# Early loads reordered over two queues, residual stores on GpSimd's queue, rotary products and low parts on VectorE in a two-layer decoder step

## The chip, the cores and the metric

The kernel runs on one core of one Trainium2 chip. The metric is the device time of one execution in microseconds (us). The engines are PE (TensorE), DVE (VectorE), ACT (ScalarE), POOL (GpSimd) and SP (SyncE, which only issues transfers here). An engine runs its instructions in one fixed row; a transfer is issued by an engine (SP, ACT or POOL), and an instruction that waits holds up everything behind it in that engine's row.

## The reference

One step of a decoder with two layers on 1024 prompt tokens and 8 sequences of 4 new tokens, 1056 tokens in all, with a model width of 1024, in float32. Layer 0 mixes by multi-head latent attention, where the 32 new tokens also attend over 8192 past positions each, held in pages of 128 rows that a table names. Layer 1 mixes by a gated delta rule with a short convolution. Each layer ends with a SwiGLU network.

```python
def rmsnorm(x, w): ...            # x * rsqrt(mean(x*x) + eps) * w
def mla_core(q_lat, q_rope, rows, q_pos, k_pos):      # 8 heads, latent rows of 256 + 64
    s = (einsum('bqhr,bkr->bhqk', q_lat, c) + einsum('bqhp,bkp->bhqk', q_rope, kr)) * MLA_SCALE
    p = softmax(where(k_pos <= q_pos, s, -inf))
    return einsum('bhqk,bkr->bqhr', p, c)
def mla_out(o_lat, w_uv, w_o):
    o = einsum('bthr,hrv->bthv', o_lat, w_uv).reshape(b, t, 1024)
    return o @ w_o
def dn_mixer(...):                # u @ w_in, convolution of width 4, silu, l2norm of q and k,
    ...                           # chunked or recurrent gated delta rule over 8 heads,
    o = rmsnorm(o, g_out) * silu(z)
    return o.reshape(b, t, 1024) @ w_o, s, new_conv
def swiglu(u, w_in, w_out):       # 2816 hidden channels
    gu = u @ w_in
    return (silu(gu[..., :D_FF]) * gu[..., D_FF:]) @ w_out
# each layer: h += rmsnorm(mixer(rmsnorm(h))); h += rmsnorm(swiglu(rmsnorm(h)))
# past rows of the new tokens: cache_mla[j, page_table]
```

## The kernel before

**Products.** Activations lie with channels on the 128 partitions and tokens along the free dimension; the 1056 tokens are three column groups, `GRP`, of 384, 384 and 288. `gA` is the first two, `gB` the last. Every float32 product is made of three matmuls (`mm3`, L255 to L257): both factors are split into a high part, copied by ACT (L230), and a low part, the difference, on DVE (L231) or, where `lo_eng` says so, on POOL. A raw weight `w` is fetched by `raw_weight` (L237) on the queue that `self.queue` names, and split into `wh` and `wl`.

**Order of the work.** PE's row is the order in which the code is written (`self.order()`), and in one block POOL's row is too. The rows of the other engines come from a scheduler, and buffer sets ("pools", `scope`) decide which earlier tile a new tile's place belonged to, and so what a load waits for.

**Layer 0.** Projections with the rotary turn (`rotate`: L604 cos on DVE, L605 sin on POOL, L606 sum on DVE; `swap` fetches the swapped halves) and the attention of the prompt run to about 437 us. Attention writes its heads `oT` to memory. Then three things go together on PE: the decode attention over the pages (`Decode`: `scores` at L1750 and L1754, softmax at L1773, `turn` at L1789, `values` at L1806; a page's part 0 is 128x256, part 1, which the scores read, 128x320), the output projection `wo_half` over `gA`, whose operands `oh` and `ol` are the heads read back (halves of 128x768), and the first network `ffn_half` over `gA`. It runs to about 1200 us. The same stages for `gB`, with `mla_values` first, take until about 1580 us.

**Early loads.** In the block whose POOL row is written by hand, the first loads for all this stand: two weights, the pages of the first two decode steps (`pages(step, part, first, last)`, two transfers a page tile) and the heads. A place can be loaded when the attention is through with it. Later pages are fetched one step ahead, part 0 by POOL and part 1 by SP (L1721).

**Boundaries.** Between sublayers `boundary` takes a column group of sums `acc`, eight tiles: it fetches the residual block `hld` (L327, `NHL` = 3 buffers), scales and adds (L328, L329), stores the new residual from ACT's queue (L331), squares (L385, L389), yields to other work `1 + self.slack` times, sums the squares on PE (L406) and makes the next operands (L336, L337).

**Layer 1.** From about 1580 to 2410 us run the delta rule's eight heads. Each takes four input weights, whose low parts POOL makes (32 in all), a convolution (L1378) and a chain of small operations on DVE up to `kd` (L1668), which PE transposes (L1670). The output projection and the second network follow, to 3230 us.

Of the kernel before, what the change touches and what calls it, by code (L numbers as in the profile page):

```python
# [8 lines left out]
F32 = mybir.dt.float32  # L9
# [3 lines left out]
ALU = mybir.AluOpType  # L13
AX = mybir.AxisListType

P = 128
# [20 lines left out]
LSTEP = 4  # L37
NHL = 3
ABANK = dict(ps=1, sc=4, tp=2, po=1)
# [14 lines left out]
FIRST = 0, 3, 6  # L54
TA = GRP[2][0]
RATE = 0.55
BLK = [(i * P, min(P, T - i * P)) for i in range((T + P - 1) // P)]
# [12 lines left out]
class Two:  # L70
# [16 lines left out]
    def load(self, eng, src, halves=(0, 1)):  # L87
        for i in halves:
            t = self.half(i)
            eng.dma_start(t.bitcast(F32), src[:, (0, TA)[i]:(TA, T)[i]])  # L90

# [10 lines left out]
class K:  # L102


    def __init__(self, ctx, tc, I, O):
# [4 lines left out]
        self.pace, self.ticks = 1, 0  # L110
        self.queue = tc.nc.sync
        self.job_bank = "ps"
# [25 lines left out]
    def half(self, pool, i, dt, s, n=16):  # L138
        return pool.tile([P, (TA, T - TA)[i]], dt, tag="H", bufs=n, name=self.nm(s))

# [172 lines left out]
    def boundary_group(self, g, acc, h_src, h_dst, post, pre, u, sq, full):  # L313
# [10 lines left out]
        for k, a in enumerate(acc):  # L324
            if post is not None:
                h = self.work([P, 384], "hld", NHL)
                nc.sync.dma_start(h[:, :tn], h_src[k][:, s])  # L327
                nc.vector.scalar_tensor_tensor(a, a, self.norm_col(*post, k), r1[:, :tn], op0=ALU.mult, op1=ALU.mult)  # L328
                nc.vector.tensor_tensor(a, a, h[:, :tn], op=ALU.add)  # L329
                if h_dst is not None:  # L330
                    nc.scalar.dma_start(h_dst[k][:, s], a)  # L331
            if full:
# [7 lines left out]
        if not full:  # L340
            return
        for _ in range(1 + self.slack):
            yield 1
# [37 lines left out]
    def sumsq1(self, sums, a, tn, tag, apart=False):  # L381

        new = apart or not sums
        q = self.work([P, 384], tag if new else "sq1")
        self.nc.scalar.activation(q[:, :tn], a, AF.Square)  # L385
        if new:
            sums.append(q)
        else:
            self.nc.vector.tensor_tensor(sums[-1][:, :tn], sums[-1][:, :tn], q[:, :tn], op=ALU.add)  # L389
# [99 lines left out]
    def ffn_half(self, layer, u, r2, acc, gs, end, flush=None, full=()):  # L489
# [3 lines left out]
        def epilogue(g, p, a, hid):  # L493
# [7 lines left out]
            if g not in full:  # L501
                x = a[:, :tn] if gate else self.fp.tile([P, 384], F32, tag="fb", bufs=2, name=self.nm("fb"))[:, :tn]
                nc.vector.tensor_tensor(x, p[:, :tn], r2[:, s], op=ALU.mult)
# [97 lines left out]
    def rotate(self, raw, sw, cos, sin):  # L601

        nc = self.nc
        nc.vector.tensor_tensor(raw, raw, cos, op=ALU.mult)  # L604
        nc.gpsimd.tensor_tensor(sw, sw, sin, op=ALU.mult)  # L605
        nc.vector.tensor_tensor(raw, raw, sw, op=ALU.add)  # L606
# [27 lines left out]
    def first_layer(self, right, top, h1, h2):  # L634
# [4 lines left out]
        with ExitStack() as left:  # L639
# [23 lines left out]
            with self.banks(**DBANK):  # L663
                with self.order(mybir.EngineType.Pool):
# [4 lines left out]

                    def heads(eng, *hs, ds=(0, 1)):  # L670
                        for h in hs:
                            for d in ds:
                                eng.dma_start(uo[h][d].half(0).bitcast(F32), oT[h][d][:, :TA])
# [10 lines left out]
                    heads(nc.gpsimd, 0, ds=(1,))  # L684
                    pages(0, 0, 2, 4)
                    pages(1, 0, 0, 4)
                    pages(0, 0, 0, 1)
                    heads(nc.gpsimd, 0, ds=(0,))
                    heads(nc.sync, 6, 7)
                    for _ in range(2):  # L690
# [21 lines left out]
        self.ab = [None, top.enter_context(self.scope("ab", "right"))]  # L712
        with self.weights(*FW[1], side="left"), self.order(), self.banks(ps=8), self.scope("ffn", "right") as self.fp:
            self.queue = nc.gpsimd
            for h, x in enumerate(uo):
                for d in range(2):
                    nc.sync.dma_start(x[d].half(1)[:, :TP - TA].bitcast(F32), oT[h][d][:, TA:])
            next(steps)
            with self.scope("vals") as vals:
                self.mla_values(OL, uo, vals)  # L720
            with self.scope("ab") as self.ab[0]:
                self.wo_half(uo, acc, gB, start)
                for _ in steps:
                    pass
                for _ in self.ffn_half(0, u, r2, hid, gB, end, full=full):
                    pass
        self.kstep, self.pace, self.queue = KSTEP[0], 1, nc.sync
        return out[:2]
# [17 lines left out]

    def mla_values(self, OL, uo, wk):

        nc = self.nc
        ws = [wk.tile([P, 512], F32, tag="uv", bufs=4, name=self.nm("uv")) for _ in range(4)]  # L750
        for p, w in enumerate(ws):
            nc.sync.dma_start(w, self.I["mla_w_uv"][p])
        for h4 in (0, 4):
            ps = self.psum()
            for k in range(2):
                for e in range(4):
                    h = h4 + e
                    nc.tensor.matmul(ps[e * TS_:(e + 1) * TS_, :P], OL[:, k * 256 + h * TS_:k * 256 + (h + 1) * TS_],
                                     ws[h // 2][:, k * 256 + h % 2 * P:][:, :P], start=k == 0, stop=k == 1)
            t = wk.tile([P, P], F32, tag="ov", bufs=2, name=self.nm("ov"))  # L760
            nc.scalar.activation(t, ps[:, :P], AF.Copy)
# [668 lines left out]
    def dn_vz(self, h, st, u, r2, wk):  # L1430
# [6 lines left out]
        for c0 in (0, 4, 8):  # L1437
# [246 lines left out]
class Decode:  # L1684
# [24 lines left out]

    def load(self, i, part, c0, c1):  # L1710

        self.get(self.early[i], part, c0, c1, self.nc.gpsimd, mybir.EngineType.Pool)

    def get(self, step, part, c0, c1, eng, engine):
        I, (qd, t), (x, n) = self.k.I, step, PGP[part]
        tab = self.tab.rearrange("o (b p) -> o b p", b=DB)[:, 4 * qd + c0:4 * qd + c1, 2 * t:2 * t + 2]
        _, pages = self.nc.values_load_multi_w_load_instructions(
            tab, engines=[engine], min_val=0, max_val=I["cache"].shape[0] - 1,
            skip_runtime_bounds_check_because="the table's entries are pages of the pool")
        for i, page in enumerate(pages):  # L1720
            eng.dma_start(self.pages[step, part][c0 + i // 2][:, i % 2],  # L1721
                          I["cache"][bass.ds(page, 1)].rearrange("o p x -> (o p) x")[:, x:x + n])

    def fetch(self, part):

        if self.coming[part]:
            step = self.coming[part].pop(0)
            self.take(step, part)
            eng = (self.nc.gpsimd, mybir.EngineType.Pool), (self.nc.sync, mybir.EngineType.SP)
            self.get(step, part, 0, 4, *eng[part])  # L1730

# [213 lines left out]
```

## Time and profile before

| | |
|---|---|
| time, median of 3 runs | 3236.57 us (3231.89 to 3242.09) |
| profiled execution | 3232.45 us, span 3230.8 us, mean granted clock 0.975 |
| busy: PE / DVE / ACT / POOL | 3057.4 / 1836.3 / 1173.7 / 564.8 us |
| transfers | 432.42 MB, mean 134 GB/s |
| page loads (L1721) on POOL | 528, 549 ns of POOL each |
| low parts of 1024 columns on POOL, 1580 to 2410 us | 32, 2429 ns each |
| residual stores on ACT (L331) | 48, 192 KB in the wide groups |

Busy times are sums over the span; PE's share of 95% leaves 173 us in which it does nothing. In the rows that follow, a group reads: line, engine, operation, out<-in, then busy time and mean of one, then the idle time ahead of them with what ended it. In a row of waits the numbers are microseconds in all, times, and the longest. In a timeline the first two numbers are start and duration.

### The profile page before, as it was taken

To read this page: it belongs to the slowest core of one execution; us is meant where nothing else is said; L and a number is where in the kernel's file an instruction comes from. 1 tells how busy PE (TensorE), PEld (TensorE's weight loads), DVE (VectorE), ACT (ScalarE), POOL (GpSimd) and SP (SyncE) were. 2 spreads that over 40 slices of the span, in tenths; PEclk is the share of its full clock that TensorE was granted. 3 is DMA by queue.
4 is the path that set the end of the run, shared out by engine and by line. 5 is a ranking of instruction groups with operands and counts; after the bars stand their busy time and mean duration, and the time that the engine had idled before them with its cause. 6 is when DMAs were issued, how large, how long until landed. Compare 5 with 4: busy or idle time off the path is not lost.

```text
span 3230.8 us, 57792 instructions
## 1 busy us (share of the span) xinstructions
PE 3057.4 (95%) x21526; PEld 2805.5 (87%) x21526; DVE 1836.3 (57%) x4197; ACT 1173.7 (36%) x2547; POOL 564.8 (17%) x898
## 2 busy tenths in 40 slices
PE   8899969899999999999999999999899999999998
PEld 8878857788888888999888888888789999999997
DVE  6677745634444444796666666666577444444436
ACT  5344434553333323354344444443443111111121
POOL 1310033343334421011122222222000000000000
PEclk9999989999999999999999999999999999999998
DMA  3563269888788844275413222222332111111113
GB/s 121 189 189 100 70 222 303 278 279 270 242 256 281 262 152 161 91 228 176 134 43 87 75 66 56 74 77 57 124 125 88 40 53 42 50 41 52 40 53 108
DMA packets 287355, 432.42 MB, mean 134 GB/s; under 512 B 60449, under 2 KB 223649, under 8 KB 287074
## 3 DMA queue, kind: packets, MB, share of 16 engines
q1 hardware_dynamic: 217986, 271.75, 26.3%
q0 software_dynamic: 42992, 135.10, 13.0%
q10 hardware_dynamic: 26096, 21.86, 2.2%
q8 instruction: 170, 2.79, 0.4%
q14 instruction: 111, 0.91, 0.1%
HBM read 367.59 MB, written 58.30 MB: 132 GB/s over the span
## 4 chain that ended last, share of the span: by engine, by line
PE 77%; DVE 8%; DMA 4%; issue 3%; ACT 3%; SPq 0%; POOL 0%; ACTq 0%; POOLq 0%; DVEq 0%
PE ps L255 20%; PE ps L256 19%; PE ps L257 19%; PE po L1806 2%; PE sc L1750 2%; DVE y L1378 1%; PE tp L1054 1%; PE sc L1027 1%; DMA hld<-xT 1%; PE sc L1754 1%; PE sc L1021 1%; ACT ga L1408 1%; DMA w<-ffn_w_in 1%; ACT wh L230 1%; PE s L1624 1%
## 5 line engine op out<-in xcount | busy, mean ns | idle before, releaser
L255 PE MATMUL ps<-oh,wh 128*128 128x384 f32 (+1 forms) x2496 | 823.5, 330 | 14.1 <-ACT wh L230 13.2
L257 PE MATMUL ps<-oh,wl 128*128 128x384 f32 (+1 forms) x2496 | 808.4, 324 | 0.5 <-DVE wl L231 0.5
L256 PE MATMUL ps<-ol,wh 128*128 128x384 f32 (+1 forms) x2496 | 808.4, 324 | 0.0
L230 ACT ACTIVATE wh<-w 128x1024 fp32r<-128x1024 f32 (+3 forms) x302 | 300.6, 1003 | 669.1 <-PE ps L256 527.0
L255 PEld LDWEIGHTS ps<-oh,wh 128*128 128x128 f32 x2496 | 472.3, 189 | 45.1 <-issue 28.8
L256 PEld LDWEIGHTS ps<-ol,wh 128*128 128x128 f32 x2496 | 473.6, 190 | 0.7 <-DVE ol L231 0.3
L257 PEld LDWEIGHTS ps<-oh,wl 128*128 128x128 f32 x2496 | 472.8, 189 | 1.6 <-DVE wl L231 1.5
L231 DVE TENSOR_TENSOR wl<-w,wh 128x1024 fp32r<-128x1024 f32 (+3 forms) x267 | 307.8, 1161 | 130.8 <-ACT wh L230 127.3
L1721 POOL DMA_DIRECT2D pg<-cache x528 | 289.7, 549 | 505.9 <-PE po L1806 376.5
L255 PE MATMUL ps<-uh,wh 128*128 128x384 f32 (+1 forms) x912 | 311.2, 342 | 8.5 <-ACT wh L230 7.6
L256 PE MATMUL ps<-ul,wh 128*128 128x384 f32 (+1 forms) x912 | 312.1, 342 | 1.6 <-DVE ul L337 1.6
L257 PE MATMUL ps<-uh,wl 128*128 128x384 f32 (+1 forms) x912 | 304.7, 334 | 1.5 <-POOL wl L231 1.5
L255 PE MATMUL ps<-hh,wh 128*128 128x384 f32 (+1 forms) x880 | 294.7, 337 | 0.2 <-ACT hh L230 0.2
L256 PE MATMUL ps<-hl,wh 128*128 128x384 f32 (+1 forms) x880 | 290.6, 331 | 0.2 <-DVE hl L231 0.2
L257 PE MATMUL ps<-hh,wl 128*128 128x384 f32 (+1 forms) x880 | 289.6, 329 | 0.0
L255 PEld LDWEIGHTS ps<-uh,wh 128*128 128x128 f32 x912 | 176.1, 193 | 13.0 <-ACT wh L230 7.6
L256 PEld LDWEIGHTS ps<-ul,wh 128*128 128x128 f32 x912 | 175.9, 193 | 4.6 <-DVE ul L337 2.6
L257 PEld LDWEIGHTS ps<-uh,wl 128*128 128x128 f32 x912 | 175.6, 193 | 4.8 <-POOL wl L231 2.0
L255 PEld LDWEIGHTS ps<-hh,wh 128*128 128x128 f32 x880 | 165.8, 189 | 11.6 <-issue 7.3
L256 PEld LDWEIGHTS ps<-hl,wh 128*128 128x128 f32 x880 | 166.5, 189 | 1.4 <-DVE hl L231 0.4
L257 PEld LDWEIGHTS ps<-hh,wl 128*128 128x128 f32 x880 | 166.3, 189 | 0.1
L552 DVE TENSOR_TENSOR acc<-acc,ps 128x384 f32<-128x384 f32 (+1 forms) x240 | 121.5, 519 | 68.6 <-PE ps L257 67.7
(432 smaller groups left out, 5023.1 us busy)
## 6 DMA issues: line engine op xcount, KB each, us to landing
pg<-cache SPq DMA_DIRECT2D x496, 160.0 KB
pg<-cache POOLq DMA_DIRECT2D x512, 128.0 KB, 3.7
w<-ffn_w_in SPq DMA_DIRECT2D x86, 512.0 KB
w<-ffn_w_in POOLq DMA_DIRECT2D x52, 512.0 KB, 3.8
w<-ffn_w_out SPq DMA_DIRECT2D x40, 512.0 KB
w<-dn_w_in SPq DMA_DIRECT2D x32, 512.0 KB
w<-ffn_w_out POOLq DMA_DIRECT2D x26, 512.0 KB, 4.1
h<-acc ACTq DMA_DIRECT2D x48, 192.0 KB
```

Of the source, the lines that this page charges most:

```text
L230: self.nc.scalar.activation(hi, src, AF.Copy)
L231: (lo_eng or self.nc.vector).tensor_tensor(lo, src, hi.bitcast(F32), op=ALU.subtract)
L255: mm(out, ah, bh, start=(i == 0), stop=False)
L256: mm(out, ah, bl, start=False, stop=False)
L257: mm(out, al, bh, start=False, stop=(i == n - 1))
L552: nc.vector.tensor_tensor(acc[m][:, s], acc[m][:, s], po[:, :tn], op=ALU.add)
L1021: mm(o, qh, kh[:, c], start=True, stop=False)
L1027: mm(o, x["q2"][r, qsl], KRh[r, c], start=False, stop=True)
L1054: self.nc.tensor.transpose(ps[:, j * P:(j + 1) * P], prob[:, kb * P:(kb + 1) * P], self.ident)
L1721: eng.dma_start(self.pages[step, part][c0 + i // 2][:, i % 2], I["cache"][bass.ds(page, 1)].rearrange("o p x -> (o p) x")[:, x:x + n])
L1750: mm(row(ps, c)[:, :256].rearrange("p (g k) -> p g k", g=2), q(i, c), pgs[c][:, :, i * P:(i + 1) * P], start=i == 0, stop=False)
L1806: nc.tensor.matmul(row(po, c)[:, :256], pT[:, j * P + c * TS_:j * P + (c + 1) * TS_], v, start=j == 0, stop=t < 0 or j == 1)
```

## The change

1. **Early loads.** The order of pages and heads changes, and some go to SP. In PE's row the first values over pages move behind 13 matmuls of the output projection.
2. **Residual stores** of layer 0 go from ACT's queue to POOL's (`self.store`).
3. **Sizes.** `NHL` becomes 5 in layer 0 (3 in layer 1); `GAP` takes the place of `1 + self.slack`, with 1 in general and 3 in the `gB` stage. In PE's row the sum of squares (L406) comes 33 instructions earlier after the first group, 48 later in the `gB` stage and 22 later at the start of layer 1. The square's first tile and `fb` get one buffer instead of two.
4. **Rotary.** The product with sin moves from POOL to DVE (five of 128x1056).
5. **Low parts** of the delta rule's 32 input weights move from POOL to DVE.
6. **`mla_values`** takes its weights as eight half tiles from the pool of the `gB` sums instead of four tiles of a pool of its own.
7. **Pools** of the `gB` stage are opened in another order. In the built program the first weight load of that stage waited for PE's last matmul of the `gA` stage; now it waits for the last low part `hl` of L231 there. The third load now waits for PE's transposes that end the `gA` stage.

Lines of the changed code lie 1 to 3 further down.

```diff
-NHL = 3
+NHL = 5, 3
+GAP = 1, 3
...
-                    nc.scalar.dma_start(h_dst[k][:, s], a)
+                    self.store.dma_start(h_dst[k][:, s], a)
...
-        for _ in range(1 + self.slack):
+        for _ in range(self.gap):
             yield 1
...
-        nc.gpsimd.tensor_tensor(sw, sw, sin, op=ALU.mult)
+        nc.vector.tensor_tensor(sw, sw, sin, op=ALU.mult)
...
+                    heads(nc.sync, (6, 0), (6, 1), (7, 0))
+                    pages(1, 1, 0, 2, False)
-                    self.queue = nc.gpsimd
+                    self.queue = self.store = nc.gpsimd
...
-                    pages(0, 1, 1, 4)
-                    pages(1, 1, 0, 4)
-                    heads(nc.gpsimd, 2, 3, 4)
-                    pages(0, 1, 0, 1)
-                    pages(0, 0, 1, 2)
-                    heads(nc.gpsimd, 1, 5)
...
+                    pages(0, 1, 0, 4)
+                    pages(1, 1, 2, 3)
+                    heads(nc.gpsimd, (0, 0), (0, 1), (1, 0), (1, 1), (2, 0), (2, 1), (3, 0), (3, 1), (4, 0))
+                    pages(0, 0, 0, 3)
+                    pages(1, 1, 3, 4)
+                    pages(0, 0, 3, 4)
+                    heads(nc.sync, (7, 1))
+                    heads(nc.gpsimd, (4, 1), (5, 0), (5, 1))
                     pages(1, 0, 0, 4)
...
-            with self.scope("vals") as vals:
-                self.mla_values(OL, uo, vals)
-            with self.scope("ab") as self.ab[0]:
-                self.wo_half(uo, acc, gB, start)
...
+        with self.scope("ab") as self.ab[0], self.weights(*FW[1], side="left"), self.order(), ...
+            self.mla_values(OL, uo)
+            self.wo_half(uo, acc, gB, start)
...
-        w = self.weight(I["dn_w_in"][part], lo_eng=nc.gpsimd)
+        w = self.weight(I["dn_w_in"][part])
...
-        w = self.weight(I["dn_w_in"][24 + h], lo_eng=nc.gpsimd)
+        w = self.weight(I["dn_w_in"][24 + h])
```

POOL's row at the head of the early loads, before (`pg` are page tiles; 5062 to 5065 are the first step's part 1, 5070 to 5073 the second's; `oh` and `ol` are halves of heads). The load of pg_5063 is the one that waited for the attention's last scores:

```order
L237 DMA w_5074<-mla_w_o 128x1024
L237 DMA w_5076<-mla_w_o 128x1024
L1717 TENSOR_LOAD tab
L1721 ISA
L1721 DMA pg_5063<-cache 128x320
L1721 ISA
L1721 DMA pg_5063<-cache 128x320
```

And in the change, from the second step's page tile that POOL keeps there:

```order
L1723 DMA pg_5072<-cache 128x320
L675 DMA oh_5038<-oT_1772 128x768
L675 DMA ol_5039<-oT_1772 128x768
L675 DMA oh_5040<-oT_1773 128x768
L675 DMA ol_5041<-oT_1773 128x768
L675 DMA oh_5042<-oT_1774 128x768
L675 DMA ol_5043<-oT_1774 128x768
L675 DMA oh_5044<-oT_1775 128x768
L675 DMA ol_5045<-oT_1775 128x768
L675 DMA oh_5046<-oT_1776 128x768
```

Nine halves of heads stand ahead of the first part 0 page there, where before they stood behind all of part 1.

POOL's row at the first group's residual stores, in the change (`h_72` is the stored residual; the row before had page loads alone here):

```order
L1723 DMA pg_6054<-cache 128x256
L334 DMA h_72<-acc_5359 128x384
L334 DMA h_72<-acc_5447 128x384
L334 DMA h_72<-acc_5488 128x384
L334 DMA h_72<-acc_5618 128x384
L334 DMA h_72<-acc_5659 128x384
L1719 TENSOR_LOAD tab
L1723 ISA
L1723 DMA pg_6344<-cache 128x256
```

Five stores, each of which waits for a sum on DVE, now stand between the pages of two decode steps.

DVE's row in one delta rule head, before (`sr` and `sry` make a reciprocal root, `kd` is what PE waits for):

```order
L277 TENSOR_TENSOR nt_23290<-sry_23123 128x9
L278 SCALAR_TENSOR_TENSOR nt_23290<-nt_23290,sr_23122 128x9
L279 SCALAR_TENSOR_TENSOR sry_23123<-nt_23290,sry_23123 128x9
L1662 TENSOR_TENSOR sr_23122<-tab_22102,sry_23123 128x9
L1668 TENSOR_TENSOR kd_21763<-kd_21763,sr_23122 128x384 x2
```

And in the change:

```order
L281 SCALAR_TENSOR_TENSOR nt_23294<-nt_23294,sr_23126 128x9
L234 TENSOR_TENSOR wl_23766<-w_23763,wh_23765 128x1024
L282 SCALAR_TENSOR_TENSOR sry_23127<-nt_23294,sry_23127 128x9
L1357 TENSOR_TENSOR cb_23554<-ps_23559,R_19063 128x384
L1664 TENSOR_TENSOR sr_23126<-tab_22106,sry_23127 128x9
L1670 TENSOR_TENSOR kd_21767<-kd_21767,sr_23126 128x384 x2
```

The low part of a coming weight, and a sum of the convolution's input, now stand inside this chain.

More of the change, by code (lines that the diff above doesn't have):

```diff
@@ L55 @@
 TA = GRP[2][0]
+TB = T - TA + 8
 RATE = 0.55
@@ L89, in load @@
             t = self.half(i)
-            eng.dma_start(t.bitcast(F32), src[:, (0, TA)[i]:(TA, T)[i]])
+            eng.dma_start(t[:, :(TA, T - TA)[i]].bitcast(F32), src[:, (0, TA)[i]:(TA, T)[i]])
 def soon(f):
@@ L110, in __init__ @@
         self.pace, self.ticks = 1, 0
-        self.queue = tc.nc.sync
+        self.queue, self.store = tc.nc.sync, tc.nc.scalar
+        self.gap = GAP[0]
         self.job_bank = "ps"
@@ L325, in boundary_group @@
             if post is not None:
-                h = self.work([P, 384], "hld", NHL)
+                h = self.work([P, 384], "hld", NHL[post[0]])
                 nc.sync.dma_start(h[:, :tn], h_src[k][:, s])
@@ L383, in sumsq1 @@
         new = apart or not sums
-        q = self.work([P, 384], tag if new else "sq1")
+        q = self.work([P, 384], tag, 1 + (tag != "sqr")) if new else self.work([P, 384], "sq1")
         self.nc.scalar.activation(q[:, :tn], a, AF.Square)
@@ L712, in first_layer @@
         self.ab = [None, top.enter_context(self.scope("ab", "right"))]
-        with self.weights(*FW[1], side="left"), self.order(), self.banks(ps=8), self.scope("ffn", "right") as self.fp:
-            self.queue = nc.gpsimd
+        with self.scope("ab") as self.ab[0], self.weights(*FW[1], side="left"), self.order(), self.banks(ps=8), \
+                self.scope("ffn", "right") as self.fp:
+            self.queue, self.gap = nc.gpsimd, GAP[1]
             for h, x in enumerate(uo):
@@ L718, in first_layer @@
             next(steps)
-            with self.scope("vals") as vals:
-                self.mla_values(OL, uo, vals)
-            with self.scope("ab") as self.ab[0]:
-                self.wo_half(uo, acc, gB, start)
[L723 to L727, printed above, removed]
+            self.mla_values(OL, uo)
+            self.wo_half(uo, acc, gB, start)
+            for _ in steps:
+                pass
+            for _ in self.ffn_half(0, u, r2, hid, gB, end, full=full):
+                pass
+        self.kstep, self.pace, self.gap, self.queue, self.store = KSTEP[0], 1, GAP[0], nc.sync, nc.scalar
         return out[:2]
@@ L745, in wo_half, with mla_values @@
         self.slack = 0
-    def mla_values(self, OL, uo, wk):
+    def mla_values(self, OL, uo):
         nc = self.nc
-        ws = [wk.tile([P, 512], F32, tag="uv", bufs=4, name=self.nm("uv")) for _ in range(4)]
+        new = lambda: self.half(self.ab[0], 1, F32, "uv", 8)
+        ws = [[new(), new()] for _ in range(4)]
         for p, w in enumerate(ws):
-            nc.sync.dma_start(w, self.I["mla_w_uv"][p])
+            for k in range(2):
+                nc.sync.dma_start(w[k][:, :256], self.I["mla_w_uv"][p][:, k * 256:(k + 1) * 256])
         for h4 in (0, 4):
@@ L758, in mla_values @@
                     nc.tensor.matmul(ps[e * TS_:(e + 1) * TS_, :P], OL[:, k * 256 + h * TS_:k * 256 + (h + 1) * TS_],
-                                     ws[h // 2][:, k * 256 + h % 2 * P:][:, :P], start=k == 0, stop=k == 1)
-            t = wk.tile([P, P], F32, tag="ov", bufs=2, name=self.nm("ov"))
+                                     ws[h // 2][k][:, h % 2 * P:][:, :P], start=k == 0, stop=k == 1)
+            t = new()[:, :P]
             nc.scalar.activation(t, ps[:, :P], AF.Copy)
@@ L1708, in take, with load, get @@
         self.pages[step, part] = [self.pool.tile([P, 2, PGP[part][1]], F32, tag=f"pg{part}", bufs=PGB, name=self.k.nm("pg")) for _ in range(4)]
-    def load(self, i, part, c0, c1):
-        self.get(self.early[i], part, c0, c1, self.nc.gpsimd, mybir.EngineType.Pool)
-    def get(self, step, part, c0, c1, eng, engine):
+    def load(self, i, part, c0, c1, pool=True):
+        self.get(self.early[i], part, c0, c1, pool)
+    def get(self, step, part, c0, c1, pool):
         I, (qd, t), (x, n) = self.k.I, step, PGP[part]
@@ L1717, in get @@
         _, pages = self.nc.values_load_multi_w_load_instructions(
-            tab, engines=[engine], min_val=0, max_val=I["cache"].shape[0] - 1,
+            tab, engines=[(mybir.EngineType.SP, mybir.EngineType.Pool)[pool]], min_val=0, max_val=I["cache"].shape[0] - 1,
             skip_runtime_bounds_check_because="the table's entries are pages of the pool")
         for i, page in enumerate(pages):
-            eng.dma_start(self.pages[step, part][c0 + i // 2][:, i % 2],
+            (self.nc.sync, self.nc.gpsimd)[pool].dma_start(self.pages[step, part][c0 + i // 2][:, i % 2],
                           I["cache"][bass.ds(page, 1)].rearrange("o p x -> (o p) x")[:, x:x + n])
@@ L1728, in fetch @@
             self.take(step, part)
-            eng = (self.nc.gpsimd, mybir.EngineType.Pool), (self.nc.sync, mybir.EngineType.SP)
-            self.get(step, part, 0, 4, *eng[part])
+            self.get(step, part, 0, 4, not part)
     def scores(self):
```

16 lines of the change are left out of this document (5 added, 11 removed).

## Prediction

> **What bounds the kernel now.** I read the page's first part, then the windows by stage, then the waits of the stages in which PE is not full, and last the timelines of single holes.
>
> ```profile
> PE 3057.4 (95%) x21526; PEld 2805.5 (87%) x21526; DVE 1836.3 (57%) x4197; ACT 1173.7 (36%) x2547; POOL 564.8 (17%) x898
> ```
>
> PE is busy for 3057.4 of 3230.8 us. The change takes no matmul away, so all it can win is time in which PE stands still, 173 us, and time in which PE runs at a lower clock. The windows say where those are (the columns are length, busy time of PE, PEld, DVE, ACT, POOL, then the granted clock, the DMA share and GB/s):
>
> ```profile
> 120.00:160.00 40.00, 29.56 (x169) 28.92 (x168) 22.20 (x28) 14.91 (x35) 20.70 (x33) 0.87 0.78 271
> 400.00:440.00 40.00, 36.46 (x251) 28.55 (x250) 26.71 (x74) 19.84 (x55) 10.83 (x19) 0.99 0.31 94
> 440.00:480.00 40.00, 15.78 (x102) 13.30 (x98) 6.39 (x9) 5.14 (x11) 18.05 (x33) 0.63 0.93 337
> 520.00:560.00 40.00, 33.05 (x279) 27.70 (x278) 25.30 (x66) 17.25 (x36) 13.16 (x24) 0.87 0.96 318
> 600.00:640.00 40.00, 31.42 (x256) 25.18 (x249) 23.12 (x51) 21.30 (x37) 12.23 (x23) 0.83 0.82 267
> 800.00:1160.00 360.00, 359.54 (x3165) 303.70 (x3159) 157.53 (x314) 123.61 (x232) 146.26 (x267) 1.00 0.83 263
> 1160.00:1240.00 80.00, 74.01 (x497) 68.04 (x488) 34.77 (x60) 20.09 (x35) 11.43 (x21) 0.96 0.41 141
> 1240.00:1320.00 80.00, 73.07 (x481) 70.99 (x480) 44.86 (x102) 31.12 (x62) 7.01 (x13) 0.96 0.36 117
> 1760.00:2400.00 640.00, 595.19 (x4223) 535.55 (x4223) 396.80 (x1074) 269.67 (x742) 128.60 (x154) 0.98 0.29 84
> ```
>
> For each I take as lost the idle time plus the busy time times one minus the clock. The hole after attention, 440 to 480, loses 24.2 + 15.8 x 0.37 = 30.1 us; 520 to 560 loses 11.2; 600 to 640 loses 13.9; 1160 to 1240 loses 8.9; 1240 to 1320 loses 9.9; 120 to 160 loses 14.3; the DeltaNet heads, 1760 to 2400, lose 56.7. Between 800 and 1160 PE is full at full clock with DMA at 0.83: nothing is to be had there, only lost. The change touches all the losing places; the last 800 us keep their order.
>
> **Early loads (part 1).** These are waits between 400 and 640 us.
>
> ```profile
> POOL pg L1721 <- PE sc L1027: 59.1, 1, 59.1
> PE po L1806 <- DMA pg<-cache: 10.3, 1, 10.3
> PE sc L1750 <- DMA pg<-cache: 10.1, 1, 10.1
> PE pt L1789 <- ACT dpr L1773: 5.7, 2, 3.6
> PE ps L255 <- ACT wh L230: 8.3, 1, 8.3
> PE po L1806 <- ACT dpt L1792: 7.3, 2, 7.0
> ```
>
> POOL stands 59.1 us before one page load whose place the last attention scores hold, and every load behind it in POOL's row, the heads among them, starts only after that. DMA is at 0.31 before 440 and at 0.93 behind it. In POOL's new row all of pages(0,1), a pair of pages(1,1) and the halves of heads 0 to 4 stand ahead of the first load that the last scores hold up, and the two pairs of pages(1,1) that they do hold up went to SP. Of these I count as free before the last scores ten page loads (128x320 of 4 bytes, 160 KB each, with the pair) and 7 halves of heads (128x768, 384 KB): 4.3 MB leave the crowded stretch, and at its 337 GB/s that is 12.8 us, the small end of this term. The first decode scores then find their pages, so the 10.1 us goes down to about 1. The first values over pages now stand behind 13 matmuls of the output projection in PE's row, so the 10.3 us is no longer paid before that work starts. The softmax step behind the scores (3.6) stays. 10.1 - 1 + 10.3 = 19.4, less some tail of late heads: I take **-19**, between -13 and -26 (the whole idle time and its half clock's part).
>
> **Residual loads and stores (parts 2 and 3).** The chain through the next two holes:
>
> ```profile
> 534.54 4.22 DMA hld<-xT
> 541.25 6.50 DMA hld<-xT
> 564.28 1.00 PE po L1806 x16
> 575.71 1.00 PE po L1806 x16
> 589.09 6.13 DMA hld<-xT
> 600.91 4.65 DMA hld<-xT
> ```
>
> With three buffers, the fourth residual block is fetched only when the first is used, and the fetch takes 4 to 6.5 us; it is paid twice in each of two column groups (10.7 and 10.8 us), and PE's 7.0 and 8.3 us hang on it. With five buffers, five blocks are there beforehand and the last three are fetched while five are worked on, so one fetch at most shows, partly. Of 11.2 + 13.9 = 25.1 us lost I take **-14**; it could be nothing, if the last three fetches, which stand behind eight page loads on SP, come as late as before at a DMA share of 0.96, and at most -22. The shorter gap in gA brings the first group's sum of squares forward by 33 instructions in PE's row, some 4 us at 360 us for 3165 matmuls; with the wait for the residuals gone that is covered, without it this end becomes +4.
>
> The 48 stores go from ACT's queue to POOL's. How long an issue takes there is in these rows (issues of page loads on POOL from 430 to 640, and one store on ACT):
>
> ```profile
> L1721 POOL DMA_DIRECT2D pg<-cache x130 | 71.7, 551 | 129.2 <-PE po L1806 111.3 <-issue 9.0 <-DMA ol<-oT 1.1
> 530.08 0.34 ACTq L331 DMA_DIRECT2D h<-acc  x1
> pg<-cache POOLq DMA_DIRECT2D x512, 128.0 KB, 3.7
> ```
>
> 48 x 0.55 = 26 us of POOL, hidden as long as POOL has time: it is busy for 13 of 40 us in this stretch. But a store waits for DVE's sum in POOL's row, and page loads stand behind it: five of the first eight stand ahead of one step's pages. A decode step comes every 575.71 - 564.28 = 11.4 us; eight issues take 4.4 and a page 3.7 to land, so 3.3 us of lateness is free. I take **+4** for the two groups, between 0 and +12 (two groups late by a 6 us fetch each). The trace has no store on POOL, so the price is an estimate. The Trainium skill speaks against this move ("SBUF — State Buffer", "SBUF: two separate sides"): descriptors of a DMA issued from GpSimd are written by GpSimd itself, which certain VectorE operations lock out, so such a DMA can wait for VectorE, while one from ScalarE's queue cannot. By that the term would lie at +12 and the sum at 3189. The 551 ns issues above, with VectorE busy beside them, show little of it.
>
> **The last columns' stage (parts 3, 6 and 7).**
>
> ```profile
> 1199.02 0.56 DVE L231 TENSOR_TENSOR hl<-fa,hh 128x384 fp32r<-128x384 f32 x1
> 1214.93 1.61 POOL L237 DMA_DIRECT2D w<-ffn_w_in  x3 [41.88 <-PE ps L257]
> PE ps L255 <- ACT wh L230: 4.8, 1, 4.8
> 1297.48 4.08 DMA hld<-xT
> 1302.88 3.72 DMA hld<-xT
> PE ps L406 <- DVE sqr L389: 5.9, 1, 5.9
> ```
>
> The first weight of this stage is issued at 1214.93, when PE's last matmul of the stage before gives its place free, and PE then waits through its landing and both splits (4.8 us idle). In the new layout that load's place was last held by hl of L231, written at 1199.02: it can start 15 us earlier. At 1303 the two residual waits leave PE idle for 5.9 us; here five buffers help, and the sum of squares comes 48 instructions later in PE's row, 48 x 73.07 / 481 = 7.3 us of other work. Of 8.9 + 9.9 = 18.8 lost us I take **-12**, between -3 (only the first gap, half) and -15. The half-width tiles cost nothing that I can find: four more small loads on SP, which is idle there.
>
> **Rotary (part 4).**
>
> ```profile
> 131.48 3.43 POOL L605 TENSOR_TENSOR araw<-araw,sin 128x1056 f32<-128x1056 f32 x1 [2.61 <-issue]
> 131.35 1.26 DVE L604 TENSOR_TENSOR qr<-qr,cos 128x1056 f32<-128x1056 f32 x1 [3.31 <-issue]
> 132.52 4.21 DVE L231 TENSOR_TENSOR wl<-w,wh 128x384 fp32r<-128x384 f32 x4
> PE ps L255 <- ACT qr L847: 9.0, 1, 9.0
> ```
>
> PE waits 9.0 us for qr, which ACT copies only after its work on the rotated keys. POOL's product takes 3.43 us, DVE's of that size 1.26, and the key swap's DMA stands behind POOL's product in its row. The chain gets some 7 us shorter, but four small weight parts (4.21 us here) now follow the rotations on DVE, and PE needs them first. I take **-4.5**, between 0 and -9.
>
> **Low parts on DVE (part 5).** One of four equal places:
>
> ```profile
> 1929.20 0.17 DVE L278 SCALAR_TENSOR_TENSOR nt<-nt,sr 128x9 f32<-128x9 f32 x1
> 1929.40 2.38 DVE L279 SCALAR_TENSOR_TENSOR sry<-nt,sry 128x9 f32<-128x9 f32 x1
> 1929.37 2.40 POOL L231 TENSOR_TENSOR wl<-w,wh 128x1024 fp32r<-128x1024 f32 x1 [1.09 <-ACT wh L230]
> PE bp L1670 <- DVE kd L1668: 13.1, 6, 3.1
> L231 DVE TENSOR_TENSOR wl<-w,wh 128x1024 fp32r<-128x1024 f32 (+3 forms) x267 | 307.8, 1161 | 130.8 <-ACT wh L230 127.3
> ```
>
> An operation that takes 0.17 us undisturbed takes 2.38 here, for exactly as long as POOL's wl runs beside it. The kd that PE waits for comes 2.2 us late, four times with 3.1 us idle. That is what the Trainium skill says ("SBUF — State Buffer", "SBUF: two separate sides"): VectorE and GpSimd lock each other out of a shared port pair for a whole instruction. The trace agrees. On DVE the same wl takes 1.16 us, and it stands inside this same chain, now in all heads: kd comes about 1 us earlier at the four places, and where POOL's wl did not meet the chain, later by up to 1.2. On DVE's whole account, 32 x 1.2 = 38 us come in and about 32 x (2.4 - 0.2) go where it was locked out; it was busy for 397 of 640. I take **-8** with the half clock that followed those four holes, between +10 (eight heads, 1.2 each, nothing won) and -15.
>
> Sizes of fb and sq: 0, since their users are DVE and ACT in row, with slack in the windows above.
>
> **Sum.** -19 - 14 + 4 - 12 - 4.5 - 8 = -53.5 against the profiled execution's 3232.45: 3179. The runs' median, 3236.57, lies 4 us above that execution, so I give **3181**.
>
> **Rivals.** (a) Bytes and not queues set the first 640 us: the share is 0.93 to 0.96 there, and loads that start sooner take the places of others. Then the first term is -13, the residual loads -3, the last columns' -12, the rotary -4.5, the low parts -4, the stores +4: 3232 - 32.5, about 3200. For it speak those shares; against it, that the two long waits stand at single loads and DMA was at 0.31 just ahead. (b) What is won at the start is lost again, because the decode steps from 480 to 1160 wait for pages that only come as fast as before: first two terms 0, the rest of the sum -20 with the low parts at +2 instead: about 3222 to 3230, no change. Against it: 359.54 of 360 us busy at a share of 0.83. (c) Slower: every wl on DVE holds PE, because DVE in its fixed row also waits for ACT's high part before it, as POOL did in the row above (1.09): 32 x (1.16 + 1.09) = 72 us against the other terms' 45.5, +26.5, about 3259. It decides from 45.5 / 32 = 1.4 us per wl. Against it: DVE would be at some 67% in that stretch, and weights are split well ahead of use. (d) More: the upper ends of the first two terms, and the half clock gone with them: about 3155.
>
> **Chances.** Forecast 0.53 (3163 to 3198), (a) 0.22, (b) 0.07, (c) 0.07, (d) 0.11. The range 3156 to 3216 holds the forecast, (d) in most of it and (a). A change under 0.3%, 10 us, cannot be told from none here: faster 0.86, same 0.07, slower 0.07.
>
> **What would show it.** Right: in 440 to 480 PE busy above 30; no scores or values waiting over 3 us for pages there; no residual wait over 3 us ahead of L385; the first gB weight issued before 1205 on the old clock; qr's wait near 4; no DVE operation of 128x9 above 1.3 us beside a wl. Wrong: page waits of POOL on DVE's sum with PE's values behind them, PE waiting for wl of DVE in the heads by more than 10 us in all, or a DMA share at 0.95 and up from 440 to 640 with PE's holes only moved.

## The result and the profile after

The changed kernel takes 3183.42 us, median of 4 runs (3181.79 to 3185.63), against 3234.23 us (3228.14 to 3242.09) for the kernel before: a ratio of 0.9842, 95% interval 0.9819 to 0.9865. The forecast was 3181. A second measurement at the end gave 0.9843 (0.9819 to 0.9868). The sum was right; four of the five rows of the table below were not, in both directions.

The busy times of the profiled execution after, whose span is 3180.1 us:

```profile
PE 3062.9 (96%) x21526; PEld 2807.7 (88%) x21526; DVE 1835.7 (58%) x4234; ACT 1170.1 (37%) x2545; POOL 493.8 (16%) x897
```

PE's work is what it was, 3062.9 against 3057.4 us, and it now stands still for 117 us of the span instead of 173. DVE is busy for just as long as before, though it has taken over 37 operations from POOL. That is the first surprise, and the low parts below explain it.

Since both kernels run 21,526 matmuls, the start of the n-th one can be compared. "PE ahead" below is how much earlier it starts than in the profile before, read at the matmul that started there at the time given. Single profiles of one kernel differ by some microseconds in these numbers, so those of the repetition (experiment 12) stand beside them. The experiments that leave a stretch as it is are repetitions too: in four profiles of the unaltered places (the changed kernel, experiments 5, 6 and 12) PE gains 5.1 to 8.3 us from 480 to 640, and 11.2 to 16.8 from 430 to 640.

| stretch (old clock) | PE gains, after | repetition | forecast |
|---|---|---|---|
| 0 to 200, rotary | -1.6 | -6.1 | +4.5 |
| 430 to 480, early loads | +8.7 | +8.6 | +19 |
| 480 to 640, residual loads and stores | +5.9 | +5.4 | +14 - 4 |
| 1200 to 1320, last group's stage | +11.0 | +10.6 | +12 |
| 1560 to 2300, delta rule | +27.8 | +25.3 | +8 |
| all other stretches | -1.1 | -5.2 | 0 |
| sum | +50.7 | +38.6 | +53.5 |

The windows of the early part, after, with the columns as before:

```profile
120.00:160.00 40.00, 35.07 (x211) 34.03 (x209) 22.89 (x30) 13.66 (x33) 16.60 (x33) 0.97 0.85 298
160.00:200.00 40.00, 34.28 (x170) 28.72 (x171) 23.46 (x53) 17.71 (x45) 4.00 (x10) 0.77 0.86 276
440.00:480.00 40.00, 22.22 (x171) 18.33 (x172) 8.80 (x15) 10.38 (x21) 10.37 (x19) 0.74 0.84 278
520.00:560.00 40.00, 34.71 (x307) 29.23 (x303) 31.35 (x72) 21.09 (x47) 17.78 (x33) 0.91 0.93 314
600.00:640.00 40.00, 36.99 (x306) 31.27 (x303) 22.10 (x48) 20.07 (x31) 17.50 (x32) 0.96 0.90 295
```

And one of them in the kernel before, which the prediction does not show:

```profile
160.00:200.00 40.00, 36.47 (x215) 31.41 (x213) 26.10 (x56) 19.18 (x48) 9.57 (x13) 0.91 0.88 283
```

PE is fuller in each but one: it is busy for 35.07 us instead of 29.56 around the rotary, but from 160 to 200 for 34.28 instead of 36.47, at a granted clock of 0.77 instead of 0.91. From 440 to 480 it has 22.22 us, well under the 30 that the forecast named as the sign of its term.

### The profile page after: what moved, and what is told of

It reads as the page before. It is cut to its first block, busy times and chain, and to the rows that moved or that the text cites. A ratio compares the mean times of both kernels' runs of the same rounds, so it can differ in the third digit from the quotient of the medians.

```text
span 3180.1 us, 57805 instructions
## 1 busy us (share of the span) xinstructions
PE 3062.9 (96%) x21526; PEld 2807.7 (88%) x21526; DVE 1835.7 (58%) x4234; ACT 1170.1 (37%) x2545; POOL 493.8 (16%) x897
## 4 chain that ended last, share of the span: by engine, by line
PE 83%; DVE 8%; DMA 4%; issue 2%; ACT 2%; SPq 1%; POOL 0%; DVEq 0%; ACTq 0%; POOLq 0%
PE ps L258 21%; PE ps L260 21%; PE ps L259 21%; PE po L1807 2%; PE sc L1751 2%; PE tp L1056 1%; DMA w<-ffn_w_in 1%; PE sc L1029 1%; DVE wl L234 1%; PE sc L1755 1%; PE sc L1023 1%; PE s L1626 1%; ACT ga L1410 1%; PE s L1623 1%; DMA w<-mla_w_o 1%
## 5 line engine op out<-in xcount | busy, mean ns | idle before, releaser
L234 DVE TENSOR_TENSOR wl<-w,wh 128x1024 fp32r<-128x1024 f32 (+3 forms) x299 | 343.0, 1155 | 149.9 <-ACT wh L233 145.7
```

What stands on the lines that cost most here:

```text
L234: (lo_eng or self.nc.vector).tensor_tensor(lo, src, hi.bitcast(F32), op=ALU.subtract)
```

## Experiments

Each kernel is the changed one with one edit, unless it says otherwise, and each ratio is to the kernel before in the same series of runs. Since that kernel varied between 3220 and 3246 us, effects under about 8 us are read from the stretches and not from the ratios.

**1. Early loads in the old order.**

```diff
-                    pages(0, 1, 0, 4)
-                    pages(1, 1, 2, 3)
-                    heads(nc.gpsimd, (0, 0), (0, 1), (1, 0), (1, 1), ...
+                    pages(0, 1, 1, 4)
+                    pages(1, 1, 0, 4)
+                    heads(nc.gpsimd, 2, 3, 4)
                     ...
```

> The changed kernel with the early loads in the old order, all on POOL but the last two heads; the rest as changed. Theory: the new order is what shortened the hole between attention and output projection, by the 8.7 us that PE gains there; undone, the hole between 436 and 470 us comes back to about 26 us idle, POOL stands some 59 us before its first page load again, and the time is 3183 + 9 = 3192. Rival: the order bought nothing, since the 17.2 us wait for the softmax that is left in the hole stands there in either order; then 3183 within 3.

Ratio 0.9888 (0.9864 to 0.9912). PE loses 10.8 us between 430 and 480 against the kernel before, where the changed kernel gains 8.7: undoing the order costs the changed kernel 19.5 us there, not 8.7. The waits of PE and POOL in that stretch:

```profile
POOL pg L1725 <- PE sc L1031: 59.1, 1, 59.1
PE sc L1753 <- DMA pg<-cache: 20.7, 1, 20.7
PE po L1809 <- DMA pg<-cache: 13.2, 1, 13.2
POOL pg L1725 <- PE sc L1748: 9.9, 1, 9.9
```

The 59.1 us are back, as expected. But a second wait of 9.9 us stands behind them in POOL's row, which the kernel before did not have: in the changed layout the place of one of these pages is free only after another scores step. So the old order suits the old places, and the theory had the size of the loss wrong by half. The 19.5 us are therefore not what the order won over the kernel before; that is 8.7.

**2. Three residual buffers.** The edit is `NHL = 3, 3`.

> The changed kernel with three buffers for residual blocks in layer 0 instead of five. Theory: the fourth and later fetches show again, PE's holes near 535 and 600 us grow by 5 to 7 us in all and the one near 1300 by 4: 3192. Rival: the fetches were hidden by taking stores off ACT or by the later sum of squares, and the buffers count for nothing: 3183 within 3.

Ratio 0.9857 (0.9825 to 0.9888). Between 480 and 640 PE gains 3.1 us instead of 5.9, and PE's waits are 7.7 us for the sum of squares and 5.1 for the softmax, where the changed kernel has 5.3 and 2.8. At 1300 nothing changes: 8.1 us gained in both. The buffers are worth about 3 us, in the middle between theory and rival, and only in the first place. That is little more than the profiles differ by: with five buffers the gain is 5.1 to 8.3.

**3. Residual stores on ACT.** The edit is `self.queue = nc.gpsimd`, without `self.store`.

> The changed kernel with the residual stores of layer 0 on ACT's queue again. Theory: where the stores are issued changes nothing that PE waits for, since ACT's issue takes 0.33 us and POOL's 0.55 and neither is full: 3183 within 3. Rival one (the rule against it): on POOL they hold back page loads, so putting them back wins 4 to 12: 3171 to 3179. Rival two: on ACT they stand before squares and hold PE's sums back: 3187 to 3191.

Ratio 0.987 (0.9849 to 0.9891). PE loses 2.2 us between 480 and 640 where the changed kernel gains 5.9. Its waits there, with the stores on ACT, and then POOL's wait for the stores in the changed kernel:

```profile
PE ps L409 <- DVE sqr L392: 9.8, 1, 9.8
PE ps L258 <- ACT wh L233: 8.1, 1, 8.1
```

```profile
PE ps L409 <- DVE sqr L392: 5.3, 1, 5.3
POOL h L334 <- DVE acc L332: 7.5, 5, 2.8
```

Rival two came out: stores in ACT's row stand between squares and weight splits and hold both back, and moving them is worth some 8 us, more than the buffers. The wait of 8.1 for a split weight is the 8.3 us of the kernel before, back again though there are five buffers; with three buffers and the stores on POOL (experiment 2) it did not come back. On POOL the stores do wait, 7.5 us in five times for these sums and 5.8 in two for other work of DVE, and from 470 us to the end of the decode PE has no wait for a page.

**4. The softmax ahead of the third weight's split.**

```diff
+                with ExitStack() as behind:
+                    if early and g is gs[0] and m == 2:
+                        for mark in self.marks:
+                            behind.enter_context(self.tc.issue_after(mark))
...
```

`self.marks` are two operations of the first paged softmax step. The reason for the edit is the hole that is left after the change, seen in PE's and ACT's waits:

```profile
PE pt L1790 <- ACT dpr L1774: 17.2, 1, 17.2
ACT wh L233 <- DMA w<-mla_w_o: 15.3, 1, 15.3
```

The scores were there, since PE had done them at 444.5 us. But in ACT's and DVE's rows the split of the projection's third weight stood ahead of the softmax, and its weight landed at 458.

> The changed kernel with one order added: the split of the third output weight stands behind the first paged softmax step in ACT's and DVE's rows, where the change has it ahead. Theory: of the expected gain in the hole after attention, the missing 10 us are this split, which waits 15.3 us on ACT for its weight while the scores lie ready: PE goes on at about 449 instead of 461.6, the wait moves to the third row of the projection, at most 3 us of it, and the time is 3173 to 3175. Rival: the transfers in that stretch are the bound, and the wait only goes over to the pages or heads behind it: 3183 within 2.

Ratio 0.9822 (0.9801 to 0.9842), and PE gains 8.9 us between 430 and 480: nothing won. The 17.2 us are gone, and in their place stands another wait:

```profile
PE ps L259 <- DMA ol<-oT: 12.8, 2, 11.9
```

The rival's outcome, though not its mechanism. The transfer that PE waits for is the last half of head 7. It is issued by SP, right behind the fifth weight in SP's row (at 464.20 and 463.82 us); that weight waits for the place which the third weight's split gives free, since two raw weights fit at a time. (The expectation of experiment 7 calls it the fourth.) One late weight held PE by two ways.

**5. Low parts on POOL.** The edit gives both `self.weight` calls their `lo_eng=nc.gpsimd` again.

> The changed kernel with the 32 low parts of the delta rule's input weights on POOL again. Theory: POOL's low parts lock DVE out in the heads; from the 1700s to 2300 PE loses the 14 us again that it won there, the four 3.1 us waits for kd among them, and part of the 13.5 us won between 1560 and 1700, so 15 to 25 us more than the changed kernel, a ratio to before of 0.989 to 0.992. Rival: the gain at the start of the heads is the later sum of squares and the residual buffers, and in the heads it is only the kd places: 8 to 9 us, 0.987.

Ratio 0.9919 (0.9903 to 0.9936), 3211.29 us, and PE's lead does not grow from 1560 us to the end (21.8 there, 21.3 at the end), where the changed kernel's grows by 29.3. Nearly all of the gain in the delta rule is this one edit, most of it at the start too (4.0 us are left between 1560 and 1700, of 13.5), and the rival is out.

**6. Rotary on POOL.** The edit is `nc.gpsimd.tensor_tensor(sw, sw, sin, ...)`.

> The changed kernel with the sin products on POOL again. Theory: from 140 to 180 us the transfers are the bound (their share is 0.91 to 1.04 there in the changed kernel), so the 9 us that PE is ahead at 155 are given back by 172 whatever engine makes the product: by 200 us PE stands the same within 2 us. Rival: the chain of the rotary is the bound, as predicted, and a loss of 4.5 us is seen at 200 us.

Ratio 0.9831 (0.9807 to 0.9855). At 160 us PE is behind by 0.6 us and not ahead by 9.3; at 200 us it stands at -0.8, against -1.6 in the changed kernel. The move is worth nothing, and may cost a little: from 130 to 200 us PE's lead changes by -2.7 to +0.1 us in the eleven profiles with it, by +1.2 and -0.1 in the two without it (this one and experiment 9). What ends the stretch in the changed kernel is seen in PE's waits between 130 and 205:

```profile
PE sc L258 <- ACT wh L233: 4.6, 1, 4.6
PE ps L258 <- ACT qr L849: 3.2, 1, 3.2
```

One wait of 9.0 has become these two, and the chain behind them runs over the transfers of the queries and of the swapped halves, at a DMA share of 0.91 to 1.04 from 150 to 180. That the transfers are the cause is argued from this; no run took any of them away.

**7. Softmax and last head first.** Experiment 4, and the last half of head 7 with the others on POOL: `heads(nc.gpsimd, (4, 1), (5, 0), (5, 1), (7, 1))`.

> As the kernel with the first paged softmax step ahead of the third weight's split, and the last half of head 7 is loaded by POOL before the pages of the second step, no longer by SP behind the fourth weight, whose place that same split gives free. Theory: two waits in row hang on the third weight; with both taken away the first two rows of the output projection run from 449 us on, the idle time between 436 and 480 falls from about 19 to about 8 us, and PE is 8 to 10 us further at 480 than in the changed kernel. Rival: the transfers of that stretch (0.98 and up from 444 to 459) are the bound, the last heads come no sooner than 459 and the gain is 2 us or less.

Ratio 0.983 (0.9803 to 0.9856). The window shows the hole half closed:

```profile
440.00:480.00 40.00, 30.12 (x222) 22.62 (x225) 11.83 (x21) 11.81 (x24) 13.44 (x25) 0.87 0.93 304
```

PE is busy for 30.1 us there, where the changed kernel had 22.2, and the transfers run at 304 GB/s; the changed kernel had 278 and the kernel before 337, so on the mean of these 40 us they had room. From 430 to 640 it gains 20.8 us, 6.2 more than the changed kernel (14.6; 13.9 in the repetition, 16.8 at most in the unaltered places). The comparison at 480 alone is no use here, because rows change places on PE and 9 us come back by 520. So two waits hung on one weight, the one hid the other, and taking both away won what taking one did not. The runs (3173.98 to 3191.80) are too far apart to tell 6 us in time.

**8. Old yields.** The edit is `for _ in range(1 + self.slack)`.

> The changed kernel with the old number of yields ahead of the norm's sum: two instead of one in the wide groups' output projection, two instead of three in the last group's, one instead of three at the start of layer 1. Theory: the 5.3 us wait of the sum of squares for DVE near 533 us is the shorter gap and goes (3 to 6 us won by 640), while the wait near 1300 comes back by 4 to 6 us and that at 1555 by 4, with its half clock: 3 to 6 us slower in all. Rival: the five buffers cover all of it, and the gap counts for nothing: within 2 us at each of the three places.

Ratio 0.9839 (0.9819 to 0.9859). At the three places: PE gains 9.2 us instead of 2.0 from 520 to 560, but 8.5 instead of 5.9 over 480 to 640; it gains nothing instead of 8.1 from 1290 to 1320; at the start of layer 1 there is no difference beyond 2 us. The wait of 5.3 us for the squares between 500 and 640 is gone, and the wait for the norm behind it is longer; here in this run and then in the changed kernel:

```profile
PE ps L427 <- DVE ny L282: 9.0, 2, 5.0
```

```profile
PE ps L427 <- DVE ny L282: 2.9, 1, 2.9
```

So the longer gap is what won the last group's place, alone. That the shorter one costs anything in the wide groups by 640 is not shown: 8.5 is hardly above the 8.3 of experiment 5, which has it. The 4 us expected at 1555 did not come.

**9. Low parts on DVE alone**, as the only edit to the kernel before.

> The kernel before with one edit: the delta rule's 32 low parts on DVE. Theory: this part stands by itself and carries more than half of the whole gain: 24 to 30 us faster than before, all of it after 1580 us, ratio 0.991 to 0.9925. Rival: in the changed kernel it needed the later sum of squares and the earlier loads at the start of layer 1; alone it wins only at the four kd places and a little beside, 8 to 12 us, ratio 0.9965.

Ratio 0.9922 (0.9896 to 0.9948), 3209.88 us, 27 us faster. PE's lead is 0.1 us at 1560, 24.3 at 2300 and 21.8 at the end. The part stands by itself.

**10. An idle operation on POOL.**

```diff
         w = self.weight(I["dn_w_in"][part])
+        hi = w[0].bitcast(F32)
+        nc.gpsimd.tensor_tensor(wk.tile([P, 1024], mybir.dt.bfloat16, ...), hi, hi, op=ALU.subtract)
```

> The changed kernel, low parts on DVE, with an operation added on POOL behind each of the 32 high parts: 128x1024, two inputs from the high part, a result that nothing reads (bf16, for want of room), so POOL is busy where the old low part kept it busy and no one waits for it. Theory: what the low parts on POOL cost is that DVE is locked out while POOL runs; the 25 us or more come back, ratio 0.990 or above, with operations of 128x9 on DVE stretched to over 1.5 us beside it. Rival: the cost was that PE and the next steps got POOL's low part late (2.4 us instead of 1.2); an operation no one waits for costs under 5 us.

Ratio 0.9957 (0.9941 to 0.9974), 3223.04 us: some 36 us slower than the changed kernel in experiment 12, for 32 operations that nobody waits for. One of them, then two operations of DVE in a row, of which the first ran beside it, and one that nothing disturbed:

```profile
2109.89 2.87 POOL L1340 TENSOR_TENSOR idle<-wh 128x1024 bf16<-128x1024 f32 x1 [0.30 <-ACT wh L233]
2110.92 4.35 DVE L1382 SCALAR_TENSOR_TENSOR y<-cb,conv_w,y 128x1080 f32<-128x1080 f32 x2
1899.15 1.33 DVE L1382 SCALAR_TENSOR_TENSOR y<-cb,conv_w,y 128x1080 f32<-128x1080 f32 x1
```

The two take 4.35 instead of 2.7, all of it in the first, which takes 2.97 and ends about one undisturbed length after POOL's. The rival, that POOL's low part came late, is out as the main cause. Another rival is that the added operations hold up POOL's own later work: PE's waits for POOL in the stage come to 2.2 us in all, so that is little. The expected sign, operations of 128x9 over 1.5 us, came only in part: there are some (the longest is 1.86 us), but the convolution carries half of the stretch here (its 72 operations take 1575 ns each instead of 1379, 14 of some 30 us).

**11. Three orders mended**: experiment 7 and `GAP = 2, 3`.

> The changed kernel with three orders mended: the first paged softmax step ahead of the third weight's split, the last half of head 7 on POOL, and two yields instead of one ahead of the sum of squares in the wide groups (three in the last group as changed). Theory: the first two are worth 4 to 5 us at 640 us, as the experiment with them alone showed, the third 2 to 3 more: 6 to 8 us faster than the changed kernel. Rival: both win the same wait, and the sum is no more than one of them, 3 to 5 us.

Ratio 0.9825 (0.9801 to 0.9849), 3181.11 us beside the changed kernel's 3186.94 in the same series. From 430 to 640 PE gains 22.1 us against 14.6 and 13.9, some 8 more, which is the number expected. But experiment 7 has 20.8 without the third order, whose share of 1.3 us is not shown; the intervals of the ratios overlap, so that the kernel is faster in time is not shown either.

**12. The changed kernel again.**

> The changed kernel itself, unaltered, beside the others on the same chip. Expected: a ratio to before of 0.984, as on record, within 0.003; PE ahead by some 7 us at 480, 13 at 640, 24 at 1320 and 50 at the end, with up to 5 us less where the round trip of YT through memory near 2250 waits as it did in most of the other runs.

Ratio 0.9843 (0.9819 to 0.9868). PE's lead is 2.2, 7.6, 18.5 and 38.6 us at the four places: the same gains by stretch, less 4.5 us that this execution lost before 200 us, and about 4 us each near 2250 and 2400 that the first profile did not lose. The first was the quickest of its four runs, and this one (3193.83 us) is some 7 us above the median of its own series: the lead of the usual execution lies between the two.

## Why the prediction was right, and where it was not

**Early loads, -19: came out as -8.7.** The two waits for pages are gone, as said, but PE won less than half of the 19 us. (That undoing the order costs 19.5, the number of the sum, is chance: 9.9 us of POOL's wait there comes from the new places.) The step that failed is "The softmax step behind the scores (3.6) stays". It grew to 17.2, since ACT and DVE, whose rows are fixed, were made to split a weight that had not come. The order of ACT and DVE at that place was not in the working. Experiments 4 and 7 show that some 6 of the missing 10 us were there to be had by order alone; the rest is not settled, and with transfers at 0.93 in experiment 7 bytes may well be it. Rival (a), bytes and not queues, has -13 here; it is nearer in size, but for those 6 us it names the wrong cause.

**Residual loads -14, stores +4: together -5.9.** The sum was off by 4, and the parts had the wrong owners. The buffers are worth about 3 (experiment 2). The stores (40 went to POOL, not 48) were costed as a burden on POOL, while their move off ACT is the larger gain, 8 us (experiment 3): the step that failed counted the queue that takes the work over and not the squares and splits that stand behind it on the one that gives it up. PE's 8.3 us were hung on the fetches that the buffers bring forward; they go with the stores, whatever the buffers (experiments 2 and 3). The rule of the Trainium skill that the prediction cites against the move, that a DMA issued from GpSimd can wait for VectorE, does not show in these numbers: the page loads on POOL take 547 ns each after and 549 before, and the stores there 545 (539 to 556). The +4 us of the shorter gap, named as a bound, shows as 5.3 us of PE at the sum of squares, but what experiment 8 takes from this wait it adds at the norm behind it, so by 640 no cost is shown.

**The last columns' stage, -12: -11.0.** Right in size. PE's waits at the two places, after, and POOL's first weight load:

```profile
PE ps L258 <- ACT wh L233: 1.5, 1, 1.5
PE ps L427 <- DVE ny L282: 1.1, 1, 1.1
1186.85 0.54 POOL L240 DMA_DIRECT2D w<-ffn_w_in  x1 [26.82 <-DVE hl L234]
```

The load leaves at 1186.85 instead of 1214.93 (13 us of that is PE's lead) and waits for `hl`, as the layout said. The 8.1 us at 1300 are the gap's alone; the buffers, which the step also credited, do nothing there (experiment 2).

**Rotary, -4.5: nothing.** The chain did get shorter: the wait for qr fell to 3.2 us, near the 4 that the forecast named, and PE was 9.3 us ahead at 160. The step that failed took a stretch by its first wait. DMA was at 0.88 and 0.93 from 150 to 170 before already; that the next product there waits for what these transfers bring is argued and not shown (experiment 6).

**Low parts, -8: -28.** The mechanism was right, and the size was off by about three times (27.8 and 25.3 us in the stage, 24.2 as the only edit). The step that failed is "four times with 3.1 us idle": only the place was counted where one wait was long enough to see. The lock also stretched operations for which PE waits a little in many places. The groups of DVE in the delta rule, before and then after:

```profile
L1378 DVE SCALAR_TENSOR_TENSOR y<-cb,conv_w,y 128x1080 f32<-128x1080 f32 x72 | 107.6, 1495 | 21.1 <-ACT y L1376 20.3
L1505 DVE TENSOR_TENSOR BT<-BY,BU 66x15 f32<-66x15 f32 x16 | 10.9, 679 | 0.1
L279 DVE SCALAR_TENSOR_TENSOR sry<-nt,sry 128x9 f32<-128x9 f32 x21 | 10.2, 487 | 0.7
```

```profile
L1380 DVE SCALAR_TENSOR_TENSOR y<-cb,conv_w,y 128x1080 f32<-128x1080 f32 x72 | 99.3, 1379 | 2.5 <-ACT y L1378 1.1
L1507 DVE TENSOR_TENSOR BT<-BY,BU 66x15 f32<-66x15 f32 x16 | 2.7, 169 | 0.2
L282 DVE SCALAR_TENSOR_TENSOR sry<-nt,sry 128x9 f32<-128x9 f32 x21 | 6.9, 329 | 0.5
L234 DVE TENSOR_TENSOR wl<-w,wh 128x1024 fp32r<-128x1024 f32 x36 | 44.9, 1247 | 11.6 <-ACT wh L233 11.4
```

Taking for each group of DVE's operations in the stage its mean after from its mean before, and this times its number, the kernel before spent some 35 us on being locked out, where the prediction's account had 32 x (2.4 - 0.2) = 70; 40 us of low parts (32 of 1.25) came in for it. DVE's account is nearly even, as the busy times say, and the whole stage still got 28 us shorter. Its two windows, before and after:

```profile
1580.00:2410.00 830.00, 771.58 (x5380) 689.91 (x5380) 521.92 (x1407) 352.26 (x943) 173.78 (x205) 0.97 0.29 83
```

```profile
1555.00:2360.00 805.00, 778.12 (x5387) 694.39 (x5386) 525.40 (x1454) 351.04 (x942) 96.46 (x177) 0.97 0.29 85
```

PE stood still for 58 us there before and 27 after, with DVE as busy. The likely reason, argued and not shown, is that a stretched operation falls wherever POOL happens to run, in the chains that PE waits for too, while a low part on DVE is put by the scheduler where there is time. The chain to `kd`, into which the low part was put, bore it: PE's waits for `kd` fell from 13.1 us to 2.7. Rival (c), every low part holding PE, is out.

So the total was met because the low parts gave 20 us too much and the other terms 20 too little. That is luck in the sum, not a confirmed sum. The last step was loose too: 3179 with the 4 us by which the median lies above the profile makes 3183, not 3181.

## What to carry to other kernels

When a wait is taken away, look at the fixed rows of the engines behind it for the next thing that has not come: here the softmax stood behind a split, and the last head behind a weight, and each hid the other. When work leaves an engine, price what it did to its neighbours in both places: what an operation on GpSimd costs VectorE does not show as waiting but as small operations that take over ten times their time, and it must be summed over all of them. Before a faster chain is credited, see how full the transfers of its stretch are: here, at a share of 0.9 and more, it won nothing.

## What the runs showed of the hardware

An operation of POOL with two inputs in SBUF makes an operation of DVE that also has two wait for nearly its whole length: 2.38 us instead of 0.17 in the rows of the prediction, and in experiment 10 for an operation with no other link to it. Not every operation of DVE waits: in the kernel before, three transposes, with one input each, run beside one low part at 0.43 us each, their usual time. One input is no sure sign, though: a TENSOR_SCALAR on `tab` (L1287) takes 2.29 us beside the low part at 1638, and 0.20 just before it. Which operations wait was not tried further.

```profile
1874.04 2.39 POOL L231 TENSOR_TENSOR wl<-w,wh 128x1024 fp32r<-128x1024 f32 x1 [0.60 <-ACT wh L230]
1874.51 1.47 DVE L1546 STREAM_TRANSPOSE YT<-Y 32x256 f32<-32x256 f32 x3 [1.37 <-ACT Y L1538]
```

The Trainium skill has this ("SBUF — State Buffer", "SBUF: two separate sides"), and the trace agrees; what it amounts to here, some 36 us for 32 operations, had not been expected. In experiment 10 it is seen from the other side as well. The added operation takes 1.90 us at 1918, where DVE's next operation starts after it, and 2.87 at 2109, where DVE's low part starts 0.11 us ahead of it:

```profile
1918.41 1.90 POOL L1340 TENSOR_TENSOR idle<-wh 128x1024 bf16<-128x1024 f32 x1 [0.90 <-ACT wh L233]
2109.78 1.23 DVE L234 TENSOR_TENSOR wl<-w,wh 128x1024 fp32r<-128x1024 f32 x1 [0.48 <-ACT wh L233]
```

In 22 of the 32 DVE's low part starts 0.02 to 0.30 us ahead, and these take 2.67 to 2.95 us; of the other ten, eight take 1.89 to 1.95. So whichever of the two starts first holds up the other.
